# Way-down weights through GpSimd's DMA queue, three pairs with 12 filling triples each, and odd rows of the part of two added by DMA

## The chip, the cores and the metric

The kernel runs on one core of a Trainium2 chip. The metric is the device time of one execution in microseconds (us). All matrices are fp32; each fp32 product is three TensorE matmuls of high and low halves.

## The reference, cut to what matters

One block of a transformer, S = 512 tokens, D = 1024, F = 2816, batch 1:

```python
def rmsnorm(x, g): return x * rsqrt(mean(x * x) + eps) * g
def swiglu(h, w_gate, w_up, w_down): return (silu(h @ w_gate) * (h @ w_up)) @ w_down

x = x + 0.5 * swiglu(rmsnorm(x, norm_ffn1), w_ffn1_gate, w_ffn1_up, w_ffn1_down)     # FFN1
x = x + hybrid_mixer(rmsnorm(x, norm_mix), ...)                                       # attention
x = x + 0.5 * swiglu(rmsnorm(x, norm_ffn2), w_ffn2_gate, w_ffn2_up, w_ffn2_down)     # FFN2
return rmsnorm(x, norm_final)
```

The change touches the two feed-forward stages (FFN1 and FFN2) only.

## The kernel before, in words

The activations lie transposed: x is eight tiles ("rows") of 128 features by 512 tokens, `xs[0]` to `xs[7]`. The hidden dimension F is cut into 22 blocks of 128. A block's hidden tile `h` comes from the gate and up weights ("gu"); the way down multiplies `h` by the down weights and adds half of the result to the rows of x.

**Halves.** A product in fp32 is `mm3`: high times high, high times low, low times high (lines L95, L96, L97). ScalarE (ACT) makes a high half by a rounding copy, VectorE (DVE) the low half by a subtraction. For the gate and up weights these are `sph` (L210) and `spl` (L211), for the down weights `whi` (L83) and `wlo` (L90).

**Parts.** The 22 blocks fall into parts, `PARTS=(0, 4, 6, 10, 14, 18, 22)`: a first part of four, a *part of two* (blocks 4 and 5), then four parts of four. The first part is computed plainly. All other blocks go in *pairs*: `pair` does the gate and up products of two blocks by a Strassen-like scheme of seven products. A product is four steps, a step is six matmuls 128x256, so a pair is 28 steps, and there are nine pairs per FFN. The products accumulate in PSUM tiles `pu`, `pv`, `pw`; their moving sides are parts of x (`xo`) or prepared sums of them (`th`, `tl`). A pair loads four 512 KB weight tiles `aw` from `in_wgu` (L290, six buffers), forms four sums of them on DVE (L298), splits seven operands (L210, L211) and combines the results (L316 copies on ACT to `wc`, L320 to L339 on both engines).

**Fillings.** The way down of a part comes in *triples*: three matmuls 128x512 into a PSUM tile `pd`. A part of four has 8 x 4 = 32 triples, the part of two 8 x 2 = 16. `mixed` puts triples of parts that are done between the steps of later pairs: after step i stands a triple if `i % 28` is in `SLOTS` and the triple's part is ready, which for a part is eight steps after its last pair. With the 16 numbers of `SLOTS`, pairs 1 and 2 carry 16 triples each, pair 3 carries 8 (its first eight steps; then the triples at hand are used up), pair 4 carries 8 from its tenth step on, and each later pair 16.

**Down weights.** One 512 KB tile `raw` holds the weights of 8 triples (a *chunk*). `loads` in `down` fetches it (L369) on SyncE's queue (SP), with an order that keeps it behind the last `aw` load (`with after(self.behind_load)`). `raw`, `whi` and `wlo` have three buffers each.

**Rows.** When the triples of one row are done, `half_added` adds half of `pd` to x on DVE (L489). `half_sent` does that for even rows only; for odd rows ACT copies half of `pd` to the single tile `acc` (L495) and GpSimd (POOL) starts a DMA that adds `acc` to x (L496). Parts of four use `half_sent`, the part of two `half_added`. The last part of each FFN is handled separately.

**Order.** TensorE's order is the list of steps, written by `go`. Loads, sums and halves are emitted some steps ahead of the use, by the look-ahead table `AHEAD`. The order on the other engines is made by a scheduler from that.

Of the kernel before, what the change touches and what calls it, by code (L numbers as in the profile page):

```python
# [28 lines left out]
LEAD = 8  # L29
AHEAD = ((0, 26.0, True), (0, 22.0, False), (1, 12.8, None), (2, 8.6, None))  # L30
SLOTS = (0, 1, 2, 3, 4, 5, 6, 7, 9, 12, 15, 18, 21, 23, 25, 27)


@with_exitstack
def block_kernel(ctx: ExitStack, tc: tile.TileContext, A: dict, out: bass.AP):
# [7 lines left out]
    nc = tc.nc  # L43
# [9 lines left out]
    def pt(tag, name):  # L53

        if tag is None:
            tag = ("s", "t", "o", "mm")[turns[0] % 4]
            turns[0] += 1
        return ps.tile([128, S], F32, name=name, tag=tag, bufs=2)
# [5 lines left out]
    def chunk(shape):  # L64
        raw = wp.tile([128, 1024], F32, name="raw", tag="raw", bufs=3)
        return raw[:, :shape[0] * shape[1]].rearrange("p (a b) -> p a b", a=shape[0])
# [27 lines left out]
    def mm3(p, w, v, first, last, again=False):  # L94
        nc.tensor.matmul(p, w[0], v[0], start=first, stop=False, skip_group_check=again)  # L95
        nc.tensor.matmul(p, w[0], v[1], start=False, stop=False, skip_group_check=again)  # L96
        nc.tensor.matmul(p, w[1], v[0], start=False, stop=last, skip_group_check=again)  # L97
# [79 lines left out]
    def after(ins):  # L177
        return tc.issue_after(ins.ins if hasattr(ins, "ins") else ins)

    class Ffn:  # L180
# [180 lines left out]
        def down(self, w, fs, then, tag="mm", group=1):  # L361

            n = len(fs)
            raw, got, bank = {}, {}, {}

            def loads(c):
                raw[c] = chunk((8, 128))
                with after(self.behind_load):
                    nc.sync.dma_start(raw[c], w[c])  # L369

            def halves_of(c):
                for i, v in enumerate(halves(raw.pop(c))):
                    got[8 * c + i] = v

            def run(d, k):
                if k == 0:
                    bank[d] = pt(tag, "pd")
                mm3(bank[d], got[d * n + k], self.hs[fs[k]], k == 0, k == n - 1)

            steps, seen = [], set()  # L380
            for d0 in range(0, NK, group):
                ds = range(d0, d0 + group)
                order = [(d, k) for ks in ([range(n)] if group == 1 else [range(n - 1), range(n - 1, n)])
                         for d in ds for k in ks]
                for d, k in order:
                    c = (d * n + k) // 8
                    new = c not in seen
                    seen.add(c)
                    steps.append(Step(0.68, lambda d=d, k=k: run(d, k), (lambda c=c: loads(c)) if new else None, None,
                                      (lambda c=c: halves_of(c)) if new else None,  # L390
                                      (lambda d=d: then(d, bank.pop(d))) if k == n - 1 else None, False))
            return steps

        def mixed(self, steps, fills):

            out, fills = [], list(fills)
            for i, s in enumerate(steps):
                out.append(s)
                if i % 28 in SLOTS and fills and fills[0][0] <= i:
                    out.append(fills.pop(0)[1])  # L400
            return out + [fill for _, fill in fills]

# [85 lines left out]
    def half_added(d, p):  # L488
        nc.vector.scalar_tensor_tensor(xs[d], p, 0.5, xs[d], ALU.mult, ALU.add)  # L489
# [8 lines left out]
    with ExitStack() as ph:  # L498
        tmp = ph.enter_context(tc.tile_pool(name="tmp1", bufs=5))
        hp = ph.enter_context(tc.tile_pool(name="hp1", bufs=2))  # L500
        sp = ph.enter_context(tc.tile_pool(name="sp1", bufs=2))


        wake = pt("mm", "wake")
        for _ in range(8):
            nc.tensor.matmul(wake.rearrange("p (a b) -> p a b", a=4), ones,
                             ones.unsqueeze(1).to_broadcast([128, 4, 128]), start=True, stop=True)
        nc.scalar.activation(R[:, 0:1], eps, AF.Sqrt)
        ffn = Ffn(A["wgu1"], 0, tmp, hp, sp)
        ffn.cuts = ((0, 0),)  # L510
        for f in range(2):
            ffn.early[f, 0] = chunk((8, 128))

        def first_x(k):
            nc.sync.dma_start(xs[k], A["xT"][k * 128:(k + 1) * 128])

        def first_w(f, parts, engine):
            src = A["wgu1"][f][:, 0].rearrange("p a b c -> p (a b) c")
            for s in parts:
                engine.dma_start(ffn.early[f, 0][:, s], src[:, s])  # L520

        nc.scalar.dma_start(gcol, A["gcol"])
        first_x(0)
        first_w(0, [slice(0, 4)], nc.sync)
        first_x(1)
        first_w(0, [slice(4, 8)], nc.sync)
        first_x(2)
        first_x(3)
        first_w(1, [slice(0, 8)], nc.sync)
        for k in range(4, NK):  # L530
            first_x(k)
        ffn.early[0, 1] = chunk((8, 128))
        nc.sync.dma_start(ffn.early[0, 1], A["wgu1"][0][:, 1].rearrange("p a b c -> p (a b) c"))
        tokens = [ffn.raw().rearrange("p a b c -> p (a b c)") for _ in range(NT)]
        for i in range(NT):
            nc.sync.dma_start(tokens[i], A["x"][i * 128:(i + 1) * 128])
        make_rows, put_rows = bias_rows(hp)
        ffn.xg = [gained(k, 0) for k in range(NK)]
        ffn.behind = made[0]

        def squares_of_tokens():
            for i in range(NT):
                nc.scalar.activation(tokens[i], tokens[i], AF.Square, accum_out=ss[:, 0, i:i + 1])

        def copied_bias(i):
            h = slice(2 * i, 2 * i + 2)
            row = scr_r[h]
            with after(ffn.behind_load):
                nc.sync.dma_start(scr_t[h].rearrange("h p w -> p h w"),
                                  bass.AP(tensor=row.tensor, offset=row.offset, ap=[[0, 128], [RVW, 2], [1, RVW]]))  # L550

        def copied_cmp(a, j):
            row = scr_c[0:1, :]
            with after(ffn.behind_load):
                nc.sync.dma_start(
                    cb[a * 16:(a + 1) * 16, j],
                    bass.AP(tensor=row.tensor, offset=row.offset + 31 - 8 * j - a,
                            ap=[[CMW, 16], [16 * CMW, 8], [1, 32]]))

        xg = []  # L560

        def then(d, p):
            half_added(d, p)
            xg.append(gained(d, 1))
            squares(tmp, d, "tmp", 3)

        steps, fills = begun(ffn, A["wd1"], [
            (3, squares_of_tokens), (4, lambda: roots(0, ss[:, 0])), (5, lambda: rows_of_roots(0, "mm")),
            (13, make_rows)])
        pairs = []  # L570
        for f, end in zip(PARTS[1:], PARTS[2:]):
            fs = range(f, end)
            pairs += [step for i in fs[::2] for step in ffn.pair(i)]
            if end < NF:
                fills += [(len(pairs) + 8, step) for step in ffn.down(A["wd1"][f:], fs, half_sent if len(fs) == 4 else half_added)]
        steps += ffn.mixed(pairs, fills) + ffn.down(A["wd1"][f:], fs, then, None, 4)
        pairs[20].post.append(put_rows)
        for i in range(8):
            pairs[52 + 6 * i].post.append(lambda i=i: copied_bias(i))
            for j in range(NT):  # L580
                pairs[112 + 16 * i + 4 * j].post.append(lambda i=i, j=j: copied_cmp(i, j))
        ffn.go(steps)
# [562 lines left out]
    with ExitStack() as ph:  # L1145
# [3 lines left out]
        ffn = Ffn(A["wgu2"], 2, tmp, hp, sp)  # L1149
# [3 lines left out]
        steps, fills = begun(ffn, A["wd2a"], [  # L1153
            (2, lambda: roots(2, sums_of_squares("mm"))), (4, lambda: rows_of_roots(2, "mm"))])
        pairs = []
        for f, end in zip(PARTS[1:], PARTS[2:]):
            fs = range(f, end)
            pairs += [step for i in fs[::2] for step in ffn.pair(i)]
            if end < NF:
                fills += [(len(pairs) + 8, step) for step in ffn.down(A["wd2a"][f:], fs, half_sent if len(fs) == 4 else half_added)]  # L1160
        ffn.go(steps + ffn.mixed(pairs, fills))

        def turn_x(i, half):
# [30 lines left out]
        w = []  # L1194
# [117 lines left out]
```

## Time and the profile before

| | before |
|---|---|
| three timed runs | 984.65, 989.51, 991.32 us, median 989.51 us |
| the profiled execution | 986.73 us, its span 985.0 us |
| PE (TensorE matmul) busy | 967.6 us, 98% of the span, 6084 matmuls |
| PEld (TensorE weight load) | 860.8 us, 87% |
| DVE (VectorE) | 732.5 us, 74% |
| ACT (ScalarE) | 533.2 us, 54% |
| POOL (GpSimd) | 197.5 us, 20% |
| `raw` loads of the way down, on SP | 22 + 18 of 512 KB |
| additions of `acc` to x by DMA, on POOL | 32 of 256 KB |

A timeline row gives start and length in us, then engine, line, operation, and output<-inputs; a bracket at its end is the idle time before it and what ended it. SPq is SP's sequencer, where DMAs are issued. A row of windows gives a stretch, its length, the busy time of each engine with the count of instructions, and the granted TensorE clock (1.00 is full speed).

### The profile page before, as it was taken

The page shows a single profiled execution, that of the slowest core. Times are in us where ns is not written, and L with a number is a line of the kernel's source. Part 1 is how long each engine was busy: PE and PEld are TensorE (multiplying, and loading weights), DVE is VectorE, ACT ScalarE, POOL GpSimd, SP SyncE. Part 2 cuts the span into 40 slices and gives each one's busy share as a digit, 9 for nine tenths or more (in the row PEclk, how much of TensorE's full clock was granted, in tenths as well). Part 3 has the DMA queues.
Part 4 walks back from the last instruction along what each step waited for, and adds up shares of the span by engine and source line. Part 5 has one row for each costly group of instructions (what it writes and reads, how often), then busy time and mean ns, then how long its engine had stood idle before and what let it go on. Part 6 is the DMA issues. An engine that isn't in the chain of part 4 may idle for free. (4 is left out here: it accounts for less than half of the span.)

```text
span 985.0 us, 15927 instructions
## 1 busy us (share of the span) xinstructions
PE 967.6 (98%) x6084; PEld 860.8 (87%) x6084; DVE 732.5 (74%) x1094; ACT 533.2 (54%) x891; POOL 197.5 (20%) x329
## 2 busy tenths in 40 slices
PE   9999998999999999999999999999999999999997
PEld 7888998999999888878888888888999899999985
DVE  5967797788777576668888885777578888777853
ACT  7834344454444355577676674673444544544544
POOL 0000000000000143246666564800000000000001
PEclk9999999999999999999999999999999999999999
DMA  8723346344542335662243531462432333445212
GB/s 307 256 58 106 112 160 206 98 110 125 146 147 65 72 99 171 198 196 58 70 108 97 129 98 54 150 217 53 137 108 88 127 101 120 133 139 173 64 22 86
DMA packets 50208, 122.28 MB, mean 124 GB/s; under 512 B 10545, under 2 KB 15106, under 8 KB 50132
## 3 DMA queue, kind: packets, MB, share of 16 engines
q1 hardware_dynamic: 45380, 112.86, 36.3%
q0 software_dynamic: 4608, 8.39, 4.9%
q8 instruction: 48, 0.79, 0.3%
q14 instruction: 28, 0.23, 0.1%
q10 hardware_dynamic: 144, 0.01, 0.0%
HBM read 100.08 MB, written 5.30 MB: 107 GB/s over the span
## 5 line engine op out<-in xcount | busy, mean ns | idle before, releaser
L210 ACT ACTIVATE sph<-aw 128x1024 fp32r<-128x1024 f32 x128 | 133.3, 1057 | 128.7 <-PE pu L96 46.6
L211 DVE TENSOR_TENSOR spl<-aw,sph 128x1024 fp32r<-128x1024 f32 x128 | 155.0, 1222 | 62.7 <-ACT sph L210 62.4
L83 ACT ACTIVATE whi<-raw 128x1024 fp32r<-128x1024 f32 (+3 forms) x107 | 103.6, 971 | 100.8 <-PE pd L96 25.0
L496 POOL DMA_DIRECT2D x<-acc x32 | 27.9, 873 | 608.5 <-ACT acc L495 599.5
L90 DVE TENSOR_TENSOR wlo<-raw,whi 128x1024 fp32r<-128x1024 f32 (+3 forms) x82 | 101.6, 1242 | 47.5 <-ACT whi L83 47.1
L95 PE MATMUL pd<-h,whi 128*128 128x512 f32 x320 | 126.8, 396 | 0.3 <-DVE x L489 0.3
L96 PE MATMUL pd<-h,whi 128*128 128x512 f32 x320 | 127.0, 397 | 0.0
L97 PE MATMUL pd<-h,wlo 128*128 128x512 f32 x320 | 126.0, 394 | 0.0
L95 PE MATMUL pu<-th,sph 128*128 128x256 f32 x432 | 120.8, 280 | 3.0 <-ACT sph L210 3.0
L97 PE MATMUL pu<-th,spl 128*128 128x256 f32 x432 | 120.7, 279 | 1.5 <-DVE spl L211 1.5
L96 PE MATMUL pu<-tl,sph 128*128 128x256 f32 x432 | 120.4, 279 | 0.0
L95 PEld LDWEIGHTS pu<-th,sph 128*128 128x128 f32 x432 | 82.1, 190 | 8.5 <-ACT sph L210 3.8
L298 DVE TENSOR_TENSOR aw<-aw 128x1024 f32<-128x1024 f32 x72 | 87.7, 1218 | 0.5 <-DMA aw<-in_wgu 0.3
L96 PEld LDWEIGHTS pu<-tl,sph 128*128 128x128 f32 x432 | 82.2, 190 | 4.2
L97 PEld LDWEIGHTS pu<-th,spl 128*128 128x128 f32 x432 | 82.2, 190 | 1.9 <-DVE spl L211 1.9
L95 PE MATMUL pw<-xo,sph 128*128 128x256 f32 x288 | 79.8, 277 | 1.8 <-ACT wc L316 1.8
L97 PE MATMUL pw<-xo,spl 128*128 128x256 f32 x288 | 79.6, 276 | 0.0
L96 PE MATMUL pw<-xo,sph 128*128 128x256 f32 x288 | 79.5, 276 | 0.0
L88 POOL TENSOR_TENSOR wlo<-raw,whi 128x128 fp32r<-128x128 f32 x136 | 64.2, 506 | 57.7 <-ACT whi L83 57.5
L97 PEld LDWEIGHTS pd<-h,wlo 128*128 128x128 f32 x320 | 60.4, 189 | 13.4
L95 PEld LDWEIGHTS pd<-h,whi 128*128 128x128 f32 x320 | 60.3, 189 | 3.2 <-DVE x L489 0.7
L96 PEld LDWEIGHTS pd<-h,whi 128*128 128x128 f32 x320 | 60.4, 189 | 2.5
(251 smaller groups left out, 2519.6 us busy)
## 6 DMA issues: line engine op xcount, KB each, us to landing
aw<-in_wgu SPq DMA_DIRECT2D x72, 512.0 KB, 4.2
raw<-in_wd SPq DMA_DIRECT2D x22, 512.0 KB, 6.1
raw<-in_wd2a SPq DMA_DIRECT2D x18, 512.0 KB, 5.2
x<-acc POOLq DMA_DIRECT2D x32, 256.0 KB, 3.3
raw<-in_w_a SPq DMA_DIRECT2D x16, 512.0 KB, 4.1
raw<-in_wgu SPq DMA_DIRECT2D x15, 512.0 KB, 4.6
raw<-in_w SPq DMA_DIRECT2D x8, 512.0 KB, 4.6
kvn<-xo SPq DMA_DIRECT2D x32, 128.0 KB, 2.4
```

Of the source, the lines that this page charges most:

```text
L83: nc.scalar.activation(hi[:, s], src[:, s], AF.Copy)
L88: nc.gpsimd.tensor_tensor(lo[:, i, b], src[:, i, b], f32(hi[:, i, b]), ALU.subtract)
L90: nc.vector.tensor_tensor(lo[:, s], src[:, s], f32(hi[:, s]), ALU.subtract)
L95: nc.tensor.matmul(p, w[0], v[0], start=first, stop=False, skip_group_check=again)
L96: nc.tensor.matmul(p, w[0], v[1], start=False, stop=False, skip_group_check=again)
L97: nc.tensor.matmul(p, w[1], v[0], start=False, stop=last, skip_group_check=again)
L210: nc.scalar.activation(hi, v, AF.Copy)
L211: nc.vector.tensor_tensor(lo, v, f32(hi), ALU.subtract)
L298: nc.vector.tensor_tensor(to, x, y, op)
L496: nc.gpsimd.dma_start(xs[d], acc, accum_op=ALU.add)
```

## The change

Three edits, the same for FFN1 and FFN2:

```diff
+FEWER = (0, 1, 2, 3, 4, 5, 6, 7, 12, 16, 20, 24)
...
             def loads(c):
                 raw[c] = chunk((8, 128))
-                with after(self.behind_load):
-                    nc.sync.dma_start(raw[c], w[c])
+                nc.gpsimd.dma_start(raw[c], w[c])
...
-                if i % 28 in SLOTS and fills and fills[0][0] <= i:
+                if i % 28 in (FEWER if i < 84 else SLOTS) and fills and fills[0][0] <= i:
...
             if end < NF:
-                fills += [(len(pairs) + 8, step) for step in ffn.down(A["wd1"][f:], fs, half_sent if len(fs) == 4 else half_added)]
+                fills += [(len(pairs) + 8, step) for step in ffn.down(A["wd1"][f:], fs, half_sent)]
```

The last edit is made for `wd2a` (FFN2) too. One line is added at the top, so line numbers of the helpers rise by one: `mm3` is L96 to L98, `halves` L84 and L91, `split` L211 and L212, the `aw` load L291, the sums L299; L369, L489, L495 and L496 stay.

**TensorE, pair 3 of FFN1.** This is the pair's fourth product (S1 by T1, the first into `pw`); rows with `pd` are a triple. Before, no triple stands in this product, nor in any row from the last triple of pair 3 to the tenth step of pair 4:

```order
L97 MATMUL pw_1390<-xo_125,spl_1305 128x256
L95 MATMUL pw_1390<-xo_127,sph_1304 128x256
L96 MATMUL pw_1390<-xo_128,sph_1304 128x256
L97 MATMUL pw_1390<-xo_127,spl_1305 128x256
L95 MATMUL pw_1390<-xo_127,sph_1304 128x256
L96 MATMUL pw_1390<-xo_128,sph_1304 128x256
```

Now one triple stands in it, behind the first step, as in each of the pair's last four products:

```order
L98 MATMUL pw_1354<-xo_125,spl_1266 128x256
L96 MATMUL pd_1361<-h_894,whi_1276 128x512
L97 MATMUL pd_1361<-h_895,whi_1276 128x512
L98 MATMUL pd_1361<-h_894,wlo_1277 128x512
L96 MATMUL pw_1354<-xo_127,sph_1265 128x256
L97 MATMUL pw_1354<-xo_128,sph_1265 128x256
```

Pairs 1, 2 and 3 have 12 triples each, and pair 4 has 12 (four at its start and eight from its tenth step); from there on the two orders are the same, and the number of matmuls is unchanged.

**POOL, in the first four pairs of FFN1.** Before, its queue holds only the additions to odd rows:

```order
L496 DMA x1_71<-acc_101 128x512
L496 DMA x3_73<-acc_101 128x512
L496 DMA x5_75<-acc_101 128x512
L496 DMA x7_77<-acc_101 128x512
L496 DMA x1_71<-acc_101 128x512
```

Now the loads of the down weights stand among them, first in a row and then one between two additions:

```order
L369 DMA raw_728<-in_wd1 128x1024
L369 DMA raw_983<-in_wd1 128x1024
L369 DMA raw_1116<-in_wd1 128x1024
L496 DMA x1_71<-acc_101 128x512
L369 DMA raw_1365<-in_wd1 128x1024
L496 DMA x3_73<-acc_101 128x512
L369 DMA raw_1579<-in_wd1 128x1024
L496 DMA x5_75<-acc_101 128x512
```

On SP, where `raw` and `aw` loads took turns in these pairs, the `aw` loads are now one behind the other. All 40 loads of L369 are moved.

**DVE, in the part of two of FFN1.** Before, each row of that part has an addition on DVE; these are rows 6 and 7:

```order
L211 TENSOR_TENSOR spl_1276<-aw_970,sph_1275 128x1024
L489 SCALAR_TENSOR_TENSOR x6_76<-pd_1315,x6_76 128x512
L211 TENSOR_TENSOR spl_1305<-aw_972,sph_1304 128x1024
L298 TENSOR_TENSOR aw_970<-aw_970,aw_1029 128x1024
L320 TENSOR_TENSOR t_1351<-pv_1308,wc_1298 128x2x256
L489 SCALAR_TENSOR_TENSOR x7_77<-pd_1339,x7_77 128x512
```

Now only even rows have one, and a `wlo` of a chunk further on stands between the `spl` of pair 3:

```order
L212 TENSOR_TENSOR spl_1266<-aw_924,sph_1265 128x1024
L321 TENSOR_TENSOR t_1318<-pv_1269,wc_1258 128x2x256
L299 TENSOR_TENSOR aw_922<-aw_922,aw_991 128x1024
L91 TENSOR_TENSOR wlo_1722<-raw_1579,whi_1721 128x1024
L212 TENSOR_TENSOR spl_1305<-aw_922,sph_1304 128x1024
L212 TENSOR_TENSOR spl_1339<-aw_989,sph_1338 128x1024
L212 TENSOR_TENSOR spl_1376<-aw_991,sph_1375 128x1024
L489 SCALAR_TENSOR_TENSOR x4_74<-pd_1361,x4_74 128x512
```

More of the change, by code (lines that the diff above doesn't have):

```diff
@@ L1159, in block_kernel @@
             if end < NF:
-                fills += [(len(pairs) + 8, step) for step in ffn.down(A["wd2a"][f:], fs, half_sent if len(fs) == 4 else half_added)]
+                fills += [(len(pairs) + 8, step) for step in ffn.down(A["wd2a"][f:], fs, half_sent)]
         ffn.go(steps + ffn.mixed(pairs, fills))
```

## The prediction

> **What bounds the kernel now.** The first rows of the page say how much there is to win at all.
>
> ```profile
> span 985.0 us, 15927 instructions
> PE 967.6 (98%) x6084; PEld 860.8 (87%) x6084; DVE 732.5 (74%) x1094; ACT 533.2 (54%) x891; POOL 197.5 (20%) x329
> ```
>
> TensorE is busy for 98% of the span, and the change keeps its matmuls. So only time in which TensorE waits, or runs at a lower clock, can go. I read three views: TensorE's waits, the windows of single pairs, and the timeline around each wait.
>
> ```profile
> PE pu L95 <- ACT sph L210: 3.0, 2, 2.0
> PE pw L95 <- ACT wc L316: 1.8, 2, 1.4
> PE pu L97 <- DVE spl L211: 1.5, 2, 0.8
> ```
>
> Three of TensorE's longest waits (total, times, longest) are in the pairs, each of them twice: once per FFN. The windows run from one pair's first matmul to the next one's (us, then busy time of PE, PEld, DVE, ACT and POOL, the granted clock, DMA share, GB/s):
>
> ```profile
> 120.78:145.42 24.64, 24.64 (x194) 23.55 (x192) 22.03 (x25) 11.02 (x15) 0.00 (x0) 1.00 0.39 129
> 145.42:174.92 29.50, 26.77 (x194) 25.10 (x193) 23.30 (x24) 14.02 (x18) 0.00 (x0) 0.94 0.60 202
> 205.16:235.40 30.24, 30.24 (x217) 28.09 (x216) 23.40 (x25) 15.45 (x21) 1.73 (x2) 1.00 0.46 126
> 766.60:795.32 28.72, 26.96 (x195) 25.15 (x193) 23.66 (x26) 14.85 (x20) 0.00 (x0) 0.94 0.31 111
> ```
>
> The rows are pair 3 (28 steps, 8 triples) and pair 4 (the same count) of FFN1, pair 6 (28 steps, 16 triples), and pair 4 of FFN2. Pairs 3 and 6 have no gap on TensorE, and they give the prices: a triple takes (30.24 - 24.64) / 8 = 0.70 us, a step (24.64 - 8 x 0.70) / 28 = 0.68 us. **Pair 4 loses 29.50 - 24.64 = 4.86 us in FFN1 and 28.72 - 24.64 = 4.08 us in FFN2.** Where, the timeline of pair 4 in FFN1 shows:
>
> ```profile
> 158.17 0.39 PE L97 MATMUL pd<-h,wlo 128*128 128x512 f32 x1
> 160.53 0.38 PE L95 MATMUL pu<-th,sph 128*128 128x256 f32 x1 [1.98 <-ACT sph L210]
> 160.75 0.28 PE L96 MATMUL pu<-tl,sph 128*128 128x256 f32 x1
> 161.79 0.38 PE L97 MATMUL pu<-th,spl 128*128 128x256 f32 x1 [0.76 <-DVE spl L211]
> 163.11 0.41 PE L95 MATMUL pu<-th,sph 128*128 128x256 f32 x1
> 163.32 0.41 PE L96 MATMUL pu<-tl,sph 128*128 128x256 f32 x1
> ```
>
> TensorE waits for both halves of the fifth operand, and shortly after matmuls start 0.21 us apart (163.11, 163.32), where a step's 0.68 us over six matmuls makes 0.113. So the loss has two pieces: 2.13 and 0.93 us of late starts (160.53 - 158.17 - 0.235, where 0.235 is a third of a triple; 161.79 - 160.75 - 0.113), and the remaining 1.8 us is the lower clock.
>
> The operand is late because DVE ran out of lead. In pairs 3 and 4 without the stalls DVE has 22.03 + 23.30 = 45.3 us of work for 2 x 24.64 = 49.3 us of matmuls, 92%; in pair 6 it has 23.40 for 30.24, 77%. Pairs 3 and 4 have little TensorE work for the same splitting, sums and combining.
>
> The third loss is in pair 1, and begins on SP:
>
> ```profile
> 64.27 5.85 SPq L290 DMA_DIRECT2D aw<-in_wgu  x2
> 70.18 0.42 SPq L369 DMA_DIRECT2D raw<-in_wd  x1
> ```
> ```profile
> 78.05 1.06 ACT L83 ACTIVATE whi<-raw 128x1024 fp32r<-128x1024 f32 x1 [4.88 <-DMA raw<-in_wd]
> 79.01 1.04 ACT L210 ACTIVATE sph<-aw 128x1024 fp32r<-128x1024 f32 x1
> 79.96 0.58 ACT L316 ACTIVATE wc<-pw 128x512 f32<-128x512 f32 x1
> ```
> ```profile
> 78.90 0.28 PE L97 MATMUL pu<-th,spl 128*128 128x256 f32 x1
> 80.59 0.39 PE L95 MATMUL pw<-xo,sph 128*128 128x256 f32 x1 [1.41 <-ACT wc L316]
> ```
>
> Two `aw` loads hold SP for 5.85 us, since their buffers aren't free; the `raw` load stands behind them and goes out at 70.18. ACT then waits 4.88 us for it with `whi` first in its queue, so the copy `wc` that frees a PSUM tile comes late, and TensorE starts 80.59 - 78.90 - 0.11 = **1.58 us** late. FFN2 has the same at 703 us, shorter:
>
> ```profile
> 700.81 1.06 ACT L83 ACTIVATE whi<-raw 128x1024 fp32r<-128x1024 f32 x1 [3.89 <-DMA raw<-in_wd2a]
> 702.66 0.28 PE L97 MATMUL pu<-th,spl 128*128 128x256 f32 x1
> 703.36 0.39 PE L95 MATMUL pw<-xo,sph 128*128 128x256 f32 x1 [0.42 <-ACT wc L316]
> ```
>
> That is 703.36 - 702.66 - 0.11 = **0.59 us**. TensorE's list of waits names no other place of weight in the pairs. The sum of what can go is 4.86 + 4.08 + 1.58 + 0.59 = **11.1 us**.
>
> **The change part by part.** *The queue.* These are the rows for its prices:
>
> ```profile
> L369 SPq DMA_DIRECT2D raw<-in_wd x22: 328/424/1442, 27.8 to 309.5; - x22
> L496 POOL DMA_DIRECT2D x<-acc x32: 852/866/1024, 58.4 to 955.0; - x32
> raw<-in_wd SPq DMA_DIRECT2D x22, 512.0 KB, 6.1
> x<-acc POOLq DMA_DIRECT2D x32, 256.0 KB, 3.3
> POOL x L496 <- ACT acc L495: 599.5, 31, 74.3
> ```
>
> SP loses 40 issues of 0.42 us (median, ns in the row), which nobody waits for by themselves. POOL gains 40 issues. A load from POOL's queue doesn't stand in the trace. By the additions it takes 0.87 us; by its bytes, which are double, up to 1.7. I take 0.87, 35 us in all, from the nearest row, the only one on POOL. POOL has 1.73 us of work in a whole pair (pair 6), so either hides there. Landing takes between 3.3 us (the additions) and 6.1 us (the loads from SP); neither matters where the load is asked for early, and it is: a load now waits only for one of three `raw` buffers and for what stands ahead of it on POOL. What may stand ahead is an addition that waits for ACT (599.5 us in 31 waits; 74.3 the longest). In the new order the load behind an addition serves a chunk one or two further on, so that ACT comes to that addition's `acc` before it needs the load. I price the queue at nothing added, and 1.58 + 0.59 us taken away. Behind the `aw` loads, which no longer wait for `raw` loads on SP, nothing is late next. If the cover is gone, a late load costs what it did at 78 us: 1.58 us each time.
>
> [...]
>
> *The spread.* Pairs 1 and 2 hand four triples each to pairs 3 and 4. Those have then 24.64 + 4 x 0.70 = 27.4 us of TensorE work, as pairs 1 and 2 have, and the sum over the four is the same. The rows on DVE:
>
> ```profile
> L90 DVE TENSOR_TENSOR wlo<-raw,whi 128x1024 fp32r<-128x1024 f32 x76 | 96.2, 1268 | 44.9 <-ACT whi L83 44.5
> L298 DVE TENSOR_TENSOR aw<-aw 128x1024 f32<-128x1024 f32 x72 | 87.7, 1218 | 0.5 <-DMA aw<-in_wgu 0.3
> L489 DVE SCALAR_TENSOR_TENSOR x<-pd,x 128x512 f32<-128x512 f32 x56 | 38.5, 688 | 27.8 <-PE pd L97 27.0
> ```
>
> In pairs 3 and 4 DVE gets one `wlo` more for the eight triples more (1.27 us). All eight rows of the part of two now fall into them, where four did, but with the third edit only four are added on DVE, as before. That makes 45.3 + 1.3 = 46.6 us of work for 54.9 us of matmuls, 85%, midway between the 92% that stalls and pair 6's 77% that doesn't; DVE's spare time there goes from 4.0 to 8.3 us, and both late operands were late by 3.1 us together (2.13 + 0.93). Pairs 1 and 2 shrink to the same 27.4 us, and pass on the `wlo` that pairs 3 and 4 get. So I take 4.86 + 4.08 us as gone, the lower clock with them. The bounds are nothing (the stall moves to another operand) and all of it.
>
> *The odd rows.* Eight additions (four per FFN, 8 x 0.69 = 5.5 us of DVE) become a copy on ACT, an issue on POOL and a landing. The rows for it, the first ACT's copies, the second the landing of POOL's additions:
>
> ```profile
> L495 ACT ACTIVATE acc<-pd 128x512 f32<-128x512 f32 x32 | 18.9, 591 | 35.3 <-issue 31.1 <-PE pd L97 3.3 <-DMA x<-acc 1.0
> ```
> ```profile
> DMA to landing us min/median/max: 3.3/3.3/6.3
> ```
>
> A copy takes 0.59 us (and waited for the DMA before it 1.0 us in all), the issue 0.87, the landing 3.3, with `acc` held for about 4.8 us. In the first eight steps of a pair a triple follows each step, and odd rows are four triples apart: 4 x (0.68 + 0.70) = 5.5 us. So `acc` is just free in time. ACT has the room (11.02 of 24.64 us in pair 3). I price this at nothing on TensorE; if the landing takes 6.3 us, as the additions' longest did, ACT would stand for 6.3 + 0.87 + 0.59 - 5.5 = 2.2 us once or twice per FFN, some of it before a `wc`, up to 4 us in all.
>
> **The sum.** 986.73 - 11.1 = 975.6; I leave 0.4 us for new small waits: **976 us**. The profiled time, 986.73, is that of the execution with the span of 985.0; it lies 2.8 us under the median of 989.51; against that the forecast is 1.4% less, against the profiled one 1.1%. One per cent, 9.9 us, is about what a measurement of this kernel can tell from no change.
>
> **The rivals.**
>
> *A stall stays in pairs 3 and 4* (chance 0.20): DVE's order isn't only a matter of load. The `wlo` between two `spl` delays the second by 1.27 us, or `acc` isn't free. For it speaks that a pair's third to fifth products come with four sums (1.22 us each) in a stretch; against it, that pair 6 has the same sums and no wait. Half of 8.9 us would stay: 976 + 4.5 = 980.5, with the bound from `acc` 984.
>
> *Only the waits go, the clock stays low somewhere* (0.10). The clock fell after gaps of 1.98 and 0.76 us, and I ascribe it to them. If it has another cause, 1.8 us stay in FFN1 and, taken the same way, about 2.0 in FFN2: 976 + 1.8 + 2.0 = 979.8. [...]
>
> *The change doesn't do what it says on the queue* (0.06): the loads land as late as before, because DMA engines or buffers set it. Then 2.2 us stay: 978.
>
> *Slower* (0.05): POOL's queue is served in order. If a load stands behind an addition whose `acc` waits for the row's triples, and the same triples' chunk or the one behind it needs that load, ACT waits for `whi` with `wc` and `sph` behind it. It decides from the point where a load goes out less than 6.1 + 1.06 + 1.27 = 8.4 us ahead of its first triple (landing, `whi`, `wlo`). At 1.58 us for each of the 40 chunks that would add 63 us; with every second one it is 32 us, less the 8.9 that the spread still wins: 986.7 + 32 - 8.9 = 1010. The long waits of POOL (74.3 us) speak for a queue that stands; that one addition stands per load, and a load serves eight triples (11 us of work or more), speaks against it.
>
> **How the numbers follow.** The forecast has the rest, 0.59, with its own range of 973.5 (the fastest run shown, 984.65, less 11.1) to 980 (the slowest, 991.32, less the same). The two partial cases and the stall reach to 984; with the bound of the odd rows the range is 972 to 985, and leaves out the slower case and a stall that is worse than before. Faster by over 1% holds in most of the forecast (1.1 to 1.4%) and in parts of the cases near 979, 0.57; within 1%, 0.37; slower by over 1%, 0.06.
>
> **What would show it.** In the profile after, TensorE's three waits above are gone; pairs 1 to 4 begin 27.4 us apart; the granted clock is 1.00 in pair 4; ACT no longer waits for DMAs of `raw`; L489 counts 48 and L496 40; POOL issues 40 loads at about 0.9 us. A wait of ACT for `raw` or of POOL for `acc` ahead of a load, with TensorE waiting for `wc`, would prove me wrong, and so would a wait for `spl` at another operand.

## The result, and the profile after

The changed kernel took **977.92 us** (median; 976.95 to 979.31) against 989.74 us before, a ratio of **0.989 (95% interval 0.9853 to 0.9928)**. The forecast was 976, the range 972 to 985. The profiled execution took 979.31 us, 1.4 over the median; the profiled one before lay 3.0 under its own. So the two profiles show 7.5 us less, the medians 11.8. The page after begins:

```profile
span 977.5 us, 16002 instructions
PE 964.6 (99%) x6084; PEld 859.2 (88%) x6084; DVE 730.1 (75%) x1086; ACT 537.1 (55%) x899; POOL 226.4 (23%) x377
```

The windows of pairs 1 to 4 of FFN1 and of pair 4 of FFN2 (same columns as before):

```profile
57.01:86.49 29.48, 29.31 (x211) 26.44 (x210) 19.79 (x22) 12.38 (x15) 2.92 (x4) 1.00 0.48 137
86.49:114.04 27.55, 27.55 (x206) 25.91 (x205) 22.03 (x24) 14.61 (x19) 1.51 (x3) 1.00 0.44 134
114.04:141.48 27.44, 27.44 (x206) 25.82 (x205) 24.18 (x26) 13.89 (x18) 4.47 (x6) 1.00 0.68 184
141.48:168.92 27.44, 27.44 (x206) 25.83 (x205) 22.12 (x25) 14.41 (x20) 1.46 (x3) 1.00 0.55 164
760.43:787.87 27.44, 27.44 (x207) 25.83 (x205) 22.35 (x25) 14.61 (x20) 1.48 (x3) 1.00 0.42 116
```

Both pairs 4 have TensorE busy from end to end, at a granted clock of 1.00 where it was 0.94, in the 27.44 us that were worked out. Pair 1 is longer by work that the change doesn't touch: the matmuls of the bias rows (1.47 us) and a wait of 0.34 us for a row of x, in both kernels. What TensorE still waits for anywhere, cut to the rows that matter:

```profile
PE ps_t L972 <- POOL lpn L963: 1.4, 3, 0.9
...
PE pu L96 <- DVE t L333: 0.4, 1, 0.4
...
PE pd L96 <- DVE x L489: 0.3, 2, 0.2
```

The three waits for `sph`, `wc` and `spl` are gone, and so are ACT's waits for loads of the down weights (30.6 us before). New is one of 0.4 us in pair 3 of FFN2, for a sum `t` that frees a PSUM tile; ahead of it DVE had waited 2.49 us for an `aw` load. Such waits of DVE come to 4.0 us in all, where they were 0.3. Stage by stage, worked out from the first matmul of each stage in the two traces (us):

| | before | after | difference |
|---|---|---|---|
| up to pair 1 of FFN1 | 56.52 | 57.01 | +0.49 |
| FFN1, pairs 1 to 4 | 118.40 | 111.91 | -6.49 |
| FFN1, the rest | 178.41 | 178.41 | 0.00 |
| attention, and the plain part of FFN2 | 326.98 | 329.51 | +2.53 |
| FFN2, pairs 1 to 4 | 115.01 | 111.03 | -3.98 |
| FFN2, the rest | 189.68 | 189.63 | -0.05 |
| span | 985.0 | 977.5 | -7.5 |

The pairs gave 10.47 us of the 11.1 that were forecast. Of this, 2.53 us went again in the attention stage, which no edit touches. There TensorE waited 0.93 us for `lpn`, with three short waits behind it, and the clock fell; first a window before, then the same matmuls after:

```profile
436.96:441.06 4.10, 3.17 (x19) 2.41 (x18) 2.19 (x9) 2.23 (x6) 4.10 (x8) 1.00 0.79 210
```
```profile
432.01:437.61 5.60, 4.66 (x17) 3.76 (x18) 1.58 (x7) 2.09 (x7) 4.48 (x8) 0.72 0.66 175
```

The granted clock is 0.72 in this stretch, where it was 1.00. The stretch accounts for 1.50 of the 2.53 us; the rest was not traced. On POOL, the queue shows what its entries wait for, and what a load takes to issue and to land:

```profile
POOL x L496 <- ACT acc L495: 463.1, 40, 21.7
POOL raw L369 <- DVE wlo L91: 106.0, 28, 27.2
```
```profile
L369 POOL DMA_DIRECT2D raw<-in_wd x22: 527/550/756, 28.6 to 303.8; - x22
...
DMA to landing us min/median/max: 3.7/4.1/9.4
```

Loads wait for a free buffer (`wlo` of an earlier chunk), that is, they are early. An issue takes 0.55 us, not the 0.87 taken from the additions.

### The profile page after: what moved, and what is told of

Its sections match the earlier page's. It is cut to its first block, busy times and chain, and to the rows that moved or that the text cites. A ratio compares the mean times of both kernels' runs of the same rounds, so it can differ in the third digit from the quotient of the medians.

```text
span 977.5 us, 16002 instructions
## 1 busy us (share of the span) xinstructions
PE 964.6 (99%) x6084; PEld 859.2 (88%) x6084; DVE 730.1 (75%) x1086; ACT 537.1 (55%) x899; POOL 226.4 (23%) x377
## 4 chain that ended last, share of the span: by engine, by line
PE 93%; DMA 3%; DVE 2%; POOL 1%; issue 1%; ACT 0%; SPq 0%; DVEq 0%; ACTq 0%; POOLq 0%
PE pd L96 8%; PE pd L97 8%; PE pd L98 8%; PE pu L96 7%; PE pu L98 7%; PE pu L97 7%; PE pw L96 5%; PE pw L98 5%; PE pw L97 5%; PE pp L96 3%; PE pv L98 3%; PE pv L96 3%; PE pp L98 3%; PE pv L97 3%; PE pp L97 3%; PE ps_t L972 3%
## 5 line engine op out<-in xcount | busy, mean ns | idle before, releaser
L211 ACT ACTIVATE sph<-aw 128x1024 fp32r<-128x1024 f32 x128 | 133.6, 1059 | 147.2 <-PE pu L97 61.1
L212 DVE TENSOR_TENSOR spl<-aw,sph 128x1024 fp32r<-128x1024 f32 x128 | 155.0, 1223 | 57.1 <-ACT sph L211 57.0
L84 ACT ACTIVATE whi<-raw 128x1024 fp32r<-128x1024 f32 (+3 forms) x107 | 103.7, 971 | 98.2 <-PE pd L97 53.4
L496 POOL DMA_DIRECT2D x<-acc x40 | 35.0, 875 | 463.1 <-ACT acc L495 463.1
L96 PE MATMUL pd<-h,whi 128*128 128x512 f32 x320 | 126.6, 396 | 0.3 <-DVE x L489 0.3
L98 PE MATMUL pd<-h,wlo 128*128 128x512 f32 x320 | 125.8, 393 | 0.0
L91 DVE TENSOR_TENSOR wlo<-raw,whi 128x1024 fp32r<-128x1024 f32 (+3 forms) x82 | 101.8, 1245 | 28.2 <-ACT whi L84 27.7
L96 PE MATMUL pu<-th,sph 128*128 128x256 f32 x432 | 119.5, 277 | 0.4 <-DVE t L333 0.4
L98 PE MATMUL pu<-th,spl 128*128 128x256 f32 x432 | 119.4, 276 | 0.0
L299 DVE TENSOR_TENSOR aw<-aw 128x1024 f32<-128x1024 f32 x72 | 87.8, 1219 | 4.3 <-DMA aw<-in_wgu 4.0
L96 PEld LDWEIGHTS pu<-th,sph 128*128 128x128 f32 x432 | 81.1, 188 | 4.9 <-DVE t L333 0.6
L98 PEld LDWEIGHTS pu<-th,spl 128*128 128x128 f32 x432 | 81.1, 188 | 0.0
L98 PE MATMUL pw<-xo,spl 128*128 128x256 f32 x288 | 79.6, 276 | 0.0
L96 PE MATMUL pw<-xo,sph 128*128 128x256 f32 x288 | 79.5, 276 | 0.0
L98 PEld LDWEIGHTS pd<-h,wlo 128*128 128x128 f32 x320 | 60.1, 188 | 13.3
L96 PEld LDWEIGHTS pd<-h,whi 128*128 128x128 f32 x320 | 60.1, 188 | 3.7 <-DVE x L489 0.7
```

The costliest lines, as they stand in the source:

```text
L84: nc.scalar.activation(hi[:, s], src[:, s], AF.Copy)
L91: nc.vector.tensor_tensor(lo[:, s], src[:, s], f32(hi[:, s]), ALU.subtract)
L211: nc.scalar.activation(hi, v, AF.Copy)
L212: nc.vector.tensor_tensor(lo, v, f32(hi), ALU.subtract)
L299: nc.vector.tensor_tensor(to, x, y, op)
L496: nc.gpsimd.dma_start(xs[d], acc, accum_op=ALU.add)
```

## The experiments

The profile after fits the forecast in nearly every line. But three edits were made at once, and the forecast split the gain between two of them: 2.2 us for the queue (pair 1), 8.9 us for the spread (pair 4, VectorE's amount of work). **Theory 1** is that split. **Theory 2** has one cause for all: late loads of the down weights, for which `whi` waits at the head of ACT's queue. The measure for the runs, beside the time, is the length of pairs 1 to 4, from the first matmul of pair 1 to that of pair 5 in each profile. It leaves out pair 5, which matters twice below:

| kernel | FFN1 pairs 1 to 4 | FFN2 pairs 1 to 4 | sum against before | attention | ratio of times (95%) |
|---|---|---|---|---|---|
| before | 118.40 | 115.01 | | 326.98 | |
| the whole change | 111.91 | 111.03 | -10.5 | 329.51 | 0.989 (0.9853 to 0.9928) |
| the whole change again | 112.25 | 110.92 | -10.2 | 328.13 | 0.9898 (0.9868 to 0.9928) |
| queue only | 113.23 | 111.90 | -8.3 | 327.93 | 0.9928 (0.991 to 0.9945) |
| spread only | 112.19 | 110.36 | -10.9 | 326.85 | 0.9882 (0.9867 to 0.9898) |
| odd rows only | 118.66 | 113.77 | -1.0 | 327.29 | 0.9987 (0.9974 to 0.9999) |
| without the queue | 112.35 | 110.53 | -10.5 | 329.73 | 0.9894 (0.9865 to 0.9923) |
| without the spread | 112.07 | 110.51 | -10.8 | 330.12 | 0.9887 (0.9872 to 0.9902) |
| without the odd rows | 111.93 | 110.33 | -11.2 | 326.99 | 0.9886 (0.9868 to 0.9904) |
| whole, loads early on SP | 111.90 | 110.47 | -11.0 | 326.92 | 0.9875 (0.986 to 0.9889) |
| before, loads early on SP | 114.01 | 112.19 | -7.2 | 326.51 | 0.9918 (0.9892 to 0.9944) |

### The queue alone

```diff
-                with after(self.behind_load):
-                    nc.sync.dma_start(raw[c], w[c])
+                nc.gpsimd.dma_start(raw[c], w[c])
```

> Only the loads of the down weights move to GpSimd's queue; triples and odd rows stay as before. Theory 1 (two causes: pair 1 is held by a late load, pair 4 by VectorE's load of work): the 1.58 and 0.59 us of pair 1 go, pair 4 still loses 4 to 5 us in each FFN; about 2 us less than before. Theory 2 (one cause: late loads hold ACT's queue in pair 4 as well, where whi waited 1.97 us at 153.59 and 2.51 us at 767.53): all 11 us go, about 976 us.

982.29 us, ratio 0.9928; the pairs lose 8.3 us, nearer to theory 2 than to theory 1. Pair 4 of FFN1 is 4 us shorter, at full clock:

```profile
145.47:170.92 25.45, 24.93 (x194) 23.66 (x193) 21.47 (x24) 13.17 (x18) 0.00 (x0) 1.00 0.58 187
```

How a load reaches so far shows in ACT's and DVE's timelines of pairs 3 and 4. Before:

```profile
144.10 1.06 ACT L83 ACTIVATE whi<-raw 128x1024 fp32r<-128x1024 f32 x1 [2.97 <-DMA raw<-in_wd]
153.59 1.06 ACT L83 ACTIVATE whi<-raw 128x1024 fp32r<-128x1024 f32 x1 [1.97 <-DMA raw<-in_wd]
```
```profile
145.19 1.23 DVE L90 TENSOR_TENSOR wlo<-raw,whi 128x1024 fp32r<-128x1024 f32 x1 [0.75 <-ACT whi L83]
154.69 1.23 DVE L90 TENSOR_TENSOR wlo<-raw,whi 128x1024 fp32r<-128x1024 f32 x1 [0.79 <-ACT whi L83]
```

What follows from them is the sum that the late `sph` is made of, and that `sph` itself, still before:

```profile
158.17 1.22 DVE L298 TENSOR_TENSOR aw<-aw 128x1024 f32<-128x1024 f32 x1
159.42 2.95 ACT L210 ACTIVATE sph<-aw 128x1024 fp32r<-128x1024 f32 x3 [0.86 <-DVE aw L298]
```

With the queue moved:

```profile
134.91 1.22 DVE L90 TENSOR_TENSOR wlo<-raw,whi 128x1024 fp32r<-128x1024 f32 x1
156.99 2.96 ACT L210 ACTIVATE sph<-aw 128x1024 fp32r<-128x1024 f32 x3 [1.86 <-DVE aw L298]
```

Before, two chunks came late, one ahead of pair 4 and one in it: ACT waited 2.97 and 1.97 us for them, and DVE was idle for 0.75 and 0.79 us and then spent 1.23 us on each. Behind them on DVE stand the sums of pair 4; the second ends at 159.39, ACT starts `sph` at 159.42, and TensorE waits for it until 160.53. With the queue moved, the `wlo` at 134.91 has no wait, there is none between it and 171 us, and the same `sph` starts 2.4 us earlier (both pairs 4 begin at about 145.4). The early request also lets the scheduler put the `wlo` further ahead in DVE's order; the run doesn't separate DVE's idle time from the work that left this stretch. What stays is 0.69 us in pair 4 of FFN1 and 0.92 in FFN2, late starts that wait for `spl` at full clock, and each pair 3 is 0.60 us longer than before.

### The spread alone

```diff
-                if i % 28 in SLOTS and fills and fills[0][0] <= i:
+                if i % 28 in (FEWER if i < 84 else SLOTS) and fills and fills[0][0] <= i:
```

> Only the triples are spread (12 each in the first four pairs); loads stay on SyncE's queue, and all eight rows of the part of two stay on VectorE. Theory 1: pair 4 loses at most 1 us per FFN, the wait in pair 1 stays (about 1.6 and 0.6 us); 7 to 9 us less than before. Theory 2: waits of ACT for the loads stay, and with them TensorE's stalls in pair 4; within 3 us of before.

977.77 us, ratio 0.9882: all of the gain, and the wait of pair 1 went as well, against theory 1. Theory 2, as one cause for all, falls too, since the loads are as late as they were and cost nothing in pairs 3 and 4. Pair 3, and ACT's waits for the loads:

```profile
113.76:141.20 27.44, 27.44 (x207) 25.83 (x205) 24.35 (x27) 12.22 (x15) 0.00 (x0) 1.00 0.54 165
```
```profile
ACT whi L84 <- DMA raw<-in_wd: 21.7, 10, 3.5
ACT whi L84 <- DMA raw<-in_wd2a: 13.5, 10, 2.1
```

ACT waits 35.2 us in all for loads (before 20.8 + 9.8 = 30.6), while pairs 3 and 4 show no gap on TensorE. Two new waits are in pairs 2 and 5 (0.47 and 0.89 us); ahead of the second, ACT had waited 3.39 us for a load, and DVE was busy nearly without a break from there on.

### The odd rows alone

```diff
-                fills += [... half_sent if len(fs) == 4 else half_added)]
+                fills += [... half_sent)]
```

> Only the third edit: odd rows of the part of two go by ACT and DMA, everything else as before. It takes four additions of 0.69 us per FFN off VectorE in pairs 2 and 3, 2.8 us ahead of the stall of pair 4, where the two late operands cost 3.0 us of waits in FFN1 and 2.1 us in FFN2. If VectorE's amount of work sets the stall, about 2.5 us of waits and most of the lower clock go in each FFN: 7 to 9 us less than before. If late loads of the down weights set it (queue alone took 8.3 us out of the pairs), it stays: within 3 us of before.

988.41 us, ratio 0.9987: nothing of weight. This speaks plainly against theory 1, since VectorE did lose work, in the right place. The blow isn't quite clean: the edit gives ACT a copy for each addition, and there are new waits for ACT's `wc` (0.46 us in FFN1, 1.43 in FFN2). Pairs 3 and 4 of FFN1:

```profile
121.22:145.86 24.64, 24.64 (x194) 23.56 (x193) 18.88 (x20) 12.88 (x18) 2.58 (x3) 1.00 0.60 175
145.86:175.90 30.04, 27.40 (x194) 25.32 (x193) 24.65 (x26) 14.03 (x19) 0.00 (x0) 0.94 0.55 187
```

DVE has 18.88 us of work in pair 3 where it had 22.03, and pair 4 takes 30.04 us all the same. The late chunk is still there:

```profile
144.16 1.07 ACT L83 ACTIVATE whi<-raw 128x1024 fp32r<-128x1024 f32 x1 [2.59 <-DMA raw<-in_wd]
```

### The whole change without one edit each

The three kernels are the changed one with one of the diffs above taken back.

> The whole change without the move of the loads: they stay on SyncE's queue behind the aw loads. Theory 1: as the whole change, plus the waits of pair 1 (1.6 and 0.6 us), so about 2 us over it; pair 4 runs without a gap. Theory 2: stalls of 4 to 5 us remain in pairs 3 and 4.

978.21 us; pairs 1 to 4 take as long as with the whole change (-10.5 us), not 2 us more. The spread covers the late loads of pair 1 too. But in this profile, the longest of its four executions (982.3 us), a late load costs TensorE 2.1 us in pair 5 of FFN1, which takes 32.37 us where it takes 30.24 with the whole change:

```profile
195.21 1.06 ACT L84 ACTIVATE whi<-raw 128x1024 fp32r<-128x1024 f32 x1 [5.34 <-DMA raw<-in_wd]
198.18 0.39 PE L96 MATMUL pu<-th,sph 128*128 128x256 f32 x1 [1.69 <-DVE t L333]
```

The `t` stands on DVE behind the `wlo` of that chunk. So early loads still buy something beside the spread; the medians don't show it.

> The whole change without the third edit: all eight rows of the part of two are added on VectorE, which now all fall into pairs 3 and 4. Theory 1: VectorE has 46.6 + 2.8 = 49.4 us for 54.9 us of matmuls (90%, where 92% stalled), so a wait of up to 1.5 us per FFN may come back; 0 to 3 us over the whole change. Theory 2: no difference from the whole change.

977.57 us. Here pair 3 of FFN1 has the four additions more:

```profile
114.27:141.71 27.44, 27.44 (x207) 25.82 (x205) 25.85 (x29) 12.32 (x15) 1.86 (x3) 1.00 0.52 168
```

DVE is busy for 25.85 of 27.44 us, **94%**, and TensorE has no gap. The forecast's 92% was taken over pairs 3 and 4 together; so measured this kernel has (25.85 + 22.57) / 54.88, 88%, without a gap, and odd rows alone, above, had (18.88 + 24.65) / 49.28, also 88%, with the stall. The share doesn't tell the two apart.

> The whole change without the spreading: loads on GpSimd's queue, odd rows by DMA, 16, 16, 8 and 8 triples in the first four pairs. Queue alone left waits of 0.96 us in FFN1 and 1.18 us in FFN2 for spl in pairs 3 and 4, at full clock. If those are VectorE's amount of work, the 2.8 us less of additions take them away: pairs 1 to 4 within 0.5 us of the whole change. If VectorE's order sets them, they stay.

978.07 us: with early loads and four additions less, the old packing of triples is as good as the new one. Both pairs 4 are within 0.3 us of 24.64. That fits VectorE's amount of work as the cause of the waits for `spl` that the queue alone left; the edit also changes the order of that work, so the two aren't separated.

### Early loads on SP

```diff
-                with after(self.behind_load):
-                    nc.sync.dma_start(raw[c], w[c])
+                nc.sync.dma_start(raw[c], w[c])
```

in the changed kernel (in place of its queue edit), and by itself in the kernel before:

> The whole change, but the loads of the down weights stay on SyncE's queue and are only freed from the order behind the aw loads. If what counts is that a load is asked for early, this equals the whole change. If two kinds of loads in one queue that is served in order hold each other, a raw load that waits for its buffer now delays aw loads behind it: waits of VectorE and ACT for aw, and 1 to 5 us more than the whole change.

> The kernel before with one edit: the loads of the down weights stay on SyncE's queue, freed from the order behind the aw loads. If GpSimd's queue is what helped in queue_only (8.3 us out of the pairs, 7 us of time), this stays near before. If only the early request counts, pairs 1 to 4 take about 225 us over both FFNs, as with queue alone, and the time is 982 us.

977.09 and 980.9 us: as with GpSimd's queue (977.92 and 982.29). In the first of the two, SP's queue stands much longer behind loads of `raw` (45.2 us before), and DVE waits no longer for `aw` than with the whole change (3.3 and 4.0 us):

```profile
SPq L369 <- DVE wlo L91: 244.9, 37, 16.4
SPq L291 <- DVE spl L212: 171.4, 51, 15.0
```

The other queue isn't needed; a load that isn't ordered behind the `aw` loads is.

### Late loads on POOL

```diff
-AHEAD = ((0, 26.0, True), (0, 22.0, False), ...)
+AHEAD = ((0, 26.0, True), (0, 8.7, False), ...)
...
-                nc.gpsimd.dma_start(raw[c], w[c])
+                with after(last_sent[0] or self.behind):
+                    nc.gpsimd.dma_start(raw[c], w[c])
...
-        nc.gpsimd.dma_start(xs[d], acc, accum_op=ALU.add)
+        last_sent[0] = nc.gpsimd.dma_start(xs[d], acc, accum_op=ALU.add)
```

> The changed kernel, with each load of the down weights asked for late and put behind the last addition of an odd row in GpSimd's queue (look-ahead 8.7 in place of 22). It makes the queue of the slower rival. If a load behind an addition is as dear as the late loads of before, ACT waits for raw of 2 to 5 us come back and each that is followed by wc or sph in need costs TensorE 0.6 to 1.6 us; with about a quarter of the 40 chunks hit, 6 to 16 us over the changed kernel. If the work between has room enough, under 2 us over it.

984.07 us, ratio 0.9957 (0.9938 to 0.9976) to before: some 5 to 7 us over the other runs of the change. Late loads cost, by the lower end of what was expected, and far from the 32 us that the slower rival put down for every second chunk. Two things were changed at once, the place behind an addition and the late request (a look-ahead of 8.7 us, where the forecast's sum needs 8.4), and no run has one of them alone; so that a standing queue costs this is not shown. The one profile ran at a granted clock of 0.752 throughout, so its waits can't be set beside the others; even so ACT waited for 18 loads of the down weights, 45.4 us in all.

### The whole change again

> The changed kernel once more. In its first profile the attention stage took 329.5 us against 327.0 before: TensorE waited 0.93 us for a gated product of GpSimd, then ran some 3.5 us at a lower clock. If that is chance of the loads ahead of it, this profile shows about 327 us there and a span near 975; if it belongs to the change, 329.5 again.

978.72 us; attention took 328.13 us. In all profiles of the table it lies between 326.5 and 330.1 us, and no edit sorts them: the two longest lack the queue or the spread, and those with all three have 329.5 and 328.1. The three longest (329.5, 329.7 and 330.1) are the three whose granted clock fell in that stage, at 434.51, 437.83 and 436.00 us. Which of the loads or waits ahead of that differ was not followed further.

### Gaps made on purpose

In the sixth product of pairs 5 to 9, GpSimd writes blocks of `spl` again and again, so that TensorE waits for them:

```diff
+                if name == "S4":
+                    src, (hi, lo) = A[0, 1], half[name]
+                    for k, n in enumerate(AGAIN.get((self.which, f), ())):
+                        for _ in range(n):
+                            nc.gpsimd.tensor_tensor(lo[:, k, 0], src[:, k, 0], f32(hi[:, k, 0]), ALU.subtract)
```

> The changed kernel with TensorE held up on purpose in the sixth product of pairs 5 to 9 of each FFN: GpSimd writes one 128x128 block of spl again with the same values, 13 to 20 times at 0.51 us, so that TensorE waits once in a product; in three pairs two or three shorter gaps follow each other. FFN1: gaps of about 1.4, 1.9, 2.4, 2.9 and 3.4 us; FFN2: 3.9 and 4.9 us, then pairs of gaps 0.9 and 0.7, 0.9 and 1.2, and three of 0.4, 0.7, 0.7. [...] If idle time adds up over a few us, as in before (2.0 and 0.8; 1.0 and 0.8; but not 1.4 alone), the pitch goes to 0.21 us for some 3.4 us from a single gap of about 1.7 to 2 us on, and behind the summed gaps of 1.8 and more.

The gaps came out longer, nine of 3.46 to 7.20 us and one of 2.29 at the end, and the groups of two and three gaps came as one wait each, so this run says nothing on sums. Behind each of the nine the matmuls went at half pace, 0.21 us apart where they are 0.11 us apart otherwise (behind the one of 3.98 us only from 964.71 us on, 1.3 us after its end):

```profile
194.20 0.58 PE L100 MATMUL pw<-xo,spl 128*128 128x256 f32 x1 [3.47 <-POOL spl L312]
194.58 0.41 PE L98 MATMUL pw<-xo,sph 128*128 128x256 f32 x1
194.79 0.41 PE L99 MATMUL pw<-xo,sph 128*128 128x256 f32 x1
```

> As gaps, but with shorter single gaps, since there 13 writes gave 3.47 us and each more 0.53 us: 8, 9, 10, 11 and 12 writes in pairs 5 to 9 of FFN1 should give about 0.8, 1.3, 1.9, 2.4 and 2.9 us; 11, 10, 9 and 10 in pairs 5 to 8 of FFN2 about 2.4, 1.9, 1.3 and 1.9 us. If idle time adds up over a few us, the clock stays up behind 0.8 and 1.3 us and falls from 1.9 or 2.4 us on. [...]

Eight of the gaps came out: 0.47 (twice), 1.00 (three times), 2.06, 2.39 and 2.40 us. The clock fell behind one of them only, and not behind the longest:

```profile
320.35 0.39 PE L100 MATMUL pw<-xo,spl 128*128 128x256 f32 x1 [2.06 <-POOL spl L312]
320.57 0.38 PE L98 MATMUL pw<-xo,sph 128*128 128x256 f32 x1
320.75 0.41 PE L99 MATMUL pw<-xo,sph 128*128 128x256 f32 x1
320.96 0.41 PE L100 MATMUL pw<-xo,spl 128*128 128x256 f32 x1
```
```profile
819.92 0.39 PE L100 MATMUL pw<-xo,spl 128*128 128x256 f32 x1 [2.40 <-POOL spl L312]
820.14 0.28 PE L98 MATMUL pw<-xo,sph 128*128 128x256 f32 x1
820.26 0.28 PE L99 MATMUL pw<-xo,sph 128*128 128x256 f32 x1
```

Behind 2.06 us the starts are 0.21 us apart for 3.4 us (to 323.95); behind 2.40 us they are 0.12 us apart from the second on. So the expectation doesn't hold as it was put: a gap of 2.06 us cost the clock, and those of 2.39 and 2.40 us did not.

The traces show what else counts. In this run the clock falls at 320.59 us and, at the kernel's end, at 986.19; the 665.60 us between are 195.0 times 3.413 us. In all 13 traces of the table above and of the two runs with gaps, the times between changes of the granted clock are whole multiples of 3.413 us, to within 0.001 of one. So in these traces the clock changes on a fixed grid. These are windows of that grid, around the gap of 2.06 us and then around that of 2.40 us:

```profile
317.18:320.59 3.41, 1.35 (x11) 1.11 (x10) 1.38 (x2) 0.00 (x0) 2.72 (x6) 1.00 0.00 0
320.59:324.00 3.41, 3.41 (x15) 3.12 (x15) 0.00 (x0) 0.00 (x0) 0.00 (x0) 0.50 0.00 0
```
```profile
815.53:818.94 3.41, 2.00 (x15) 1.66 (x13) 2.01 (x3) 1.06 (x1) 2.94 (x7) 1.00 0.55 154
818.94:822.35 3.41, 2.43 (x18) 2.29 (x19) 0.62 (x1) 0.00 (x0) 0.93 (x1) 1.00 0.37 131
```

The gap of 2.06 us lies in one window, and the clock is 0.50 in the next. That of 2.40 us is cut in two, 1.41 and 0.98 us, and the clock stays at 1.00. Over the windows of the 13 traces (from 25 to 960 us, those already at the low clock left out) the clock fell behind every one with 1.86 us or more of waits in it, and behind none under 1.27 us; from 1.27 to 1.83 us both occur.

## Why the prediction was right, point by point

**What can go: right.** The sum of TensorE's losses in pairs 1 and 4, 11.1 us, was read from windows and timelines. 10.5 us of it went with the whole change, and 7.2 to 11.2 us in every kernel of the table with early loads or the spread (with the loads late, 1.05 to 2.1 us came back in pair 5 of FFN1). That the 0.4 us kept for new small waits equal the wait at `t` in FFN2 is luck: no row stood behind them, and what came late there is an `aw` load, where the forecast had "nothing is late next".

**The number: right, in part by luck.** 976 starts from the profiled execution before, 986.73; from the median of 989.74 the same sum gives 979.0, still in the range. 977.92 lies between the two, with a loss of 2.5 us in the attention stage that was not forecast.

**The clock: right.** It was ascribed to the gaps, and where these went, pair 4 ran at 1.00. The rival in which the clock stays low elsewhere came true in a place that it did not name: 0.72 in the attention stage of the profiled run.

**The split over the edits: wrong.** This is the step that failed, at "The operand is late because DVE ran out of lead", with shares of 92%, 85% and 77%. Over the same two pairs 88% ran without a gap (without the odd rows) and 88% stalled (odd rows alone); and with the queue alone the share hardly fell, to (23.45 + 21.47) / 49.28 or 91%, while pair 4 of FFN1 became 4 us shorter. That the spread would bring DVE to 46.6 us in pairs 3 and 4 was right, 24.18 + 22.12 = 46.3; it was the lead, not the share, that counted. What the runs showed in its place: the stall needs two things together, late chunks (ACT's queue held by a `whi` that waits for its load, its `wlo` falling ahead of the sums in the tight stretch) and a stretch with no triples to cover them. Early loads alone take 8.3 us, the spread alone 10.9, both together 10.2 to 11.2. So the prices of these two edits can't be added; they remove the same stall.

**The queue's price: too small.** 2.2 us were put down for it, since its mark was only sought in pair 1; alone it measures 8.3. The profile held the sign: ACT's waits of 2.97 and 1.97 us for `raw` at 144.10 and 153.59, just ahead of the stall. The queue as such is not the cause; early loads on SP do the same.

**The odd rows: right as a price, wrong as a reason.** Nothing by themselves, as was said; but the spread didn't need them either. They take effect only with early loads and the old packing, where the pairs became some 2.5 us shorter (-8.3 to -10.8).

**The slower rival: right to be small.** In the changed kernel POOL did serve its queue in order: the load at 71.77 us went out 0.05 us behind an addition that had waited for ACT until 70.83. But the waits of the loads themselves are for buffers (106.0 us in 28 waits). Made to stand behind additions and asked for late, both at once, they cost 5 to 7 us.

## What to carry to other kernels

When an engine waits, look two queues back for what came late before counting how busy the engine in between is: over the same two pairs 88% busy ran without a gap in one kernel here and stalled in another. Where two edits cure the same stall by different means, late data made early or more work put over it, don't add their gains (8.3 and 10.9 us alone were 10.2 to 11.2 together here); try each alone before keeping both. A load that was ordered behind others for tidiness went out late here when those waited (5.85 us at 64.27); freed from that order it was early in the same queue as well as in another.

## What the runs showed of the hardware

- In the 13 traces the granted clock of TensorE changed on a grid of 3.413 us, and what told the gaps apart is the idle time within one window of the grid: in `gaps_short` 2.06 us in one window cost the clock for the next 3.41 us, 2.40 us cut into 1.41 and 0.98 did not. From 1.86 us in a window on it fell every time, under 1.27 us never; what decides between them is open. All nine gaps of 3.46 us and more in `gaps` cost it.
- In the profile after, a 512 KB load from GpSimd's queue took 0.55 us to issue, less than an addition of 256 KB by DMA (0.87), and landed in 4.1 us (medians).
